# A two-layer trunk on one Trainium2 core: v of the second mixer in seven block products behind the first half of u, and gate of the first FFN in block products from the third group on

## The chip, the cores and the metric

The kernel runs on one core of one Trainium2 chip. A core has TensorE (PE in the profile; its weight loads are a row of their own, PEld), VectorE (DVE), ScalarE (ACT), GpSimd (POOL) and a queue engine that issues most of the loads (SP). The metric is device time of one execution in microseconds. Each engine runs its own queue of instructions strictly in order; engines wait for each other by semaphores.

## The reference

A sequence of 512 positions with 1024 channels goes through two layers and a last norm, all in 32-bit floats. Each layer is a mixer and a gated FFN, both with a residual around them.

```python
def gated_conv_ffn(x, w_gate, w_up, conv_w, conv_b, w_down):      # D_FF = 2816
    g = causal_dwconv3(x @ w_gate, conv_w) + conv_b
    return (silu(g) * (x @ w_up)) @ w_down

# mixer of layer 1 (C_WIDTH = 1024, CHUNK = 128, 8 heads of 128 channels)
proj = gelu(rms_norm(h, norm_mix[1]) @ w_in_odd)                  # 1024 -> 2048
u, v = proj[..., :C_WIDTH], proj[..., C_WIDTH:]
vn   = rms_norm(v, sgu_norm).reshape(b, n, CHUNK, C_HEADS, C_HEAD_DIM)
gate = einsum('hts,bnshc->bnthc', w_spatial * tril, vn) + b_spatial
h    = h + (u * gate.reshape(b, s, C_WIDTH)) @ w_out_odd
```

Layer 0's mixer (a gated short convolution and multi-scale pooling) is not touched but for the pools its buffers lie in.

## The kernel before

**Products.** Every 32-bit operand is split into a high part (rounded by a copy on ScalarE) and a low part (the rest, by a subtraction). A product is three matmuls, high x high, high x low and low x high (`mm3`). The split of a weight is written in two ways: `parts` (L125 to L130) has the high part on ScalarE (L128) and the low part on VectorE (L129); `summed` (L115 to L123) has ScalarE write the negated rounded value (L120), a DMA from GpSimd's queue add the raw weight on it (L121), and ScalarE write the high part (L122). Raw weights come by SP's queue (`fetch`, L109) into four buffers; high and low parts have six each. Larger temporary sums have the tag "sum" in the stage's own pool, three buffers.

**Order.** The program is written as a sequence of calls, and a planner (a list scheduler with costs of its own) sets from it the order in each engine's queue. The changed code can therefore come out in another order than it is written in.

**Stages.** Layer 0's mixer, layer 0's FFN, layer 1's mixer, layer 1's FFN.

**FFN.** The 2816 hidden channels are 22 blocks of 128, taken in groups of two (f = 0, 2, ... 20). For each group gate and up are computed, gate goes through the causal convolution (ScalarE L506, VectorE L508) and silu (L519), is multiplied with up, and split (`act`). The table PARTS runs a down projection (`project`, 512-column matmuls, residual additions at L292) after groups 2, 4, 8, 12, 16 and 20. Three forms of a group are there:

- `direct` (groups 0 and 2): full products.
- `both` (groups 4, 6, 10, 14, 18): gate and up each in seven block products in the manner of Strassen and Winograd. The activations' block sums are made once (`normalize`); weights' block sums s12 and s34 are made per group. Each block product is 12 matmuls of 256 columns (`multiply`, L638), so a group has 2 x 84. The products of gate and up alternate; results are copied out by ScalarE (L696) or added by VectorE (L701 to L721). Three PSUM banks (a, b, e) serve each of gate and up, and are used again within the group.
- `seven` (groups 8, 12, 16, 20): up in seven block products, gate in 48 full matmuls of 512 columns.

So a `both` group has always stood behind a down projection, and a `seven` group behind a `both` group, but for group 4, which follows a down projection and is followed by one.

**Layer 1's mixer.** `in_group` computes half of v or u: 512 columns of w_in_odd, four tiles of 128 tokens, 8 x 4 x 3 = 96 matmuls of 512 columns. The order is v0, v1, then v's norm, u0, the eight spatial products, u1 with transposes between, the gating, and the output projection oo. `tail` is how many of the eight contraction steps are run tile by tile at the end (with a large tail the tiles finish one after the other, with a small one together). The spatial weights are masked by GpSimd and turned by TensorE (L877) while v0 runs, in two sets of four.

Of the kernel before, what the change touches and what calls it, by code (L numbers as in the profile page):

```python
# [8 lines left out]
F32 = mybir.dt.float32  # L9
F32R = mybir.dt.float32r  # L10
# [5 lines left out]
P = 128  # L16
# [14 lines left out]
def tile_trunk(ctx: ExitStack, tc: tile.TileContext, x, norm_mix, norm_ffn, final_norm,  # L31
# [301 lines left out]
    def mixer0():  # L333
        nonlocal prm0
        w = w_in_even[0]
        with tc.tile_pool(name="m0", bufs=1) as mp:
# [5 lines left out]
            def load(k, n):  # L342
                t = mp.tile([P, NT, n * P], F32, tag="four", bufs=5, name=f"xt{k}")
# [90 lines left out]
            def c_done(j, ps):  # L434
                if j % 2 == 0:
                    ac["pair"] = mp.tile([P, 2, S], F32, tag="four", bufs=5, name=f"ac{j}")
# [9 lines left out]
            def v_done(j, ps):  # L446
                p = padded_tile()
                nc.vector.tensor_tensor(p[:, 2:], ps, ac[j], ALU.mult)
                if j % 2 == 0:
                    cv["pair"] = mp.tile([P, 2, S], F32, tag="four", bufs=5, name=f"cv{j}")  # L450
# [37 lines left out]
    class Ffn:  # L488
# [33 lines left out]
        def act(self, ft, s):  # L522
            if ft == NF - 2 and self.kept:
                both = self.ap.tile([P, 2, S], F32R, tag="sum", bufs=3, name="a_last")
# [56 lines left out]
        def normalize(self, kp):  # L581

            n, r = f"{self.layer}_{kp}", self.r
            x = self.ap.tile([P, 2, S], F32, tag="sum", bufs=3, name=f"x{n}")
# [12 lines left out]
            t = self.ap.tile([P, 4, HALF], F32, tag="sum", bufs=3, name=f"t{n}")  # L597
            nc.vector.tensor_tensor(t[:, 1, :], b22, b12, ALU.subtract)
            nc.vector.tensor_tensor(t[:, 0, :], t[:, 1, :], b11, ALU.add)
            nc.vector.tensor_tensor(t[:, 3, :], b12, b11, ALU.subtract)  # L600
            nc.vector.tensor_tensor(t[:, 2, :], b21, t[:, 0, :], ALU.subtract)
            self.t23[kp] = self.sums(kp)
            t41 = self.ap.tile([P, 2, 2, HALF], F32R, name=f"t41_{n}")
            self.t41[kp] = t41[:, 0], t41[:, 1]
            for (hi, lo), src in ((self.t23[kp], t[:, :2, :]), (self.t41[kp], t[:, 2:, :])):
                if kp < 2:
                    halves((hi, lo), src)
                    continue
                nc.scalar.activation(lo, src, AF.Copy, scale=-1.0)
                nc.gpsimd.dma_start(lo, src, accum_op=ALU.add)  # L610
                nc.scalar.activation(hi, src, AF.Copy)
# [38 lines left out]
        def both(self, f):  # L650
# [12 lines left out]
            for key in "gu":  # L663
                r0, r1 = raws[key, 0][0], raws[key, 1][0]
                s12, s34 = (ap.tile([P, 2, 4, P], F32, tag="sum", bufs=3, name=f"{x}{key}_{n}")
                            for x in ("s12", "s34"))
# [57 lines left out]
        def seven(self, f, steps=None):  # L724
# [16 lines left out]
            gate = [parts(*raws["g", 0])]  # L741
            s23 = ap.tile([P, 2, 4, P], F32, tag="sum", bufs=3, name=f"s23_{n}")
            s14 = ap.tile([P, 2, 4, P], F32, tag="sum", bufs=3, name=f"s14_{n}")
            nc.vector.tensor_tensor(s14[:, 0], r0[:, :, P:], r1[:, :, P:], ALU.add)
# [77 lines left out]
        def hidden(self, f, before=lambda i, j: None, steps=None):  # L822
# [37 lines left out]


    def mixer1(norm):
        w = w_in_odd[0]
        with tc.tile_pool(name="m1", bufs=1) as mp:
# [6 lines left out]
                                    compare_op=ALU.is_ge, fill=0.0, base=0, channel_multiplier=1)  # L871
            wsT_hi = mp.tile([P, NK, P], F32R, name="wsT_hi")
            wsT_lo = mp.tile([P, NK, P], F32R, name="wsT_lo")
            for q in range(2):
                ps = aux_bank(f"wst{q}")
                for i in range(4):
                    nc.tensor.transpose(ps[:, i * P : (i + 1) * P], ws[:, 4 * q + i, :], ident)  # L877
                hi = wsT_hi[:, 4 * q : 4 * q + 4, :]
                pv = ps.rearrange("p (h t) -> p h t", t=P)
                nc.scalar.activation(hi, pv, AF.Copy)  # L880
                nc.vector.tensor_tensor(wsT_lo[:, 4 * q : 4 * q + 4, :], pv, hi.bitcast(F32),
                                        ALU.subtract)

# [9 lines left out]

            def v_done(half):
                def done(t, ps):
                    dst = v[t][:, half * 512 : (half + 1) * 512]
                    nc.scalar.activation(dst, ps, AF.Gelu, scale=r_of(t))
                    sq = tp.tile([P, S], F32, tag="sq", name=f"sqv{half}_{t}")
                    nc.scalar.activation(sq, dst, AF.Square, accum_out=ssv[:, half, t : t + 1])
# [18 lines left out]

            u, gt, mix = {}, {}, {}

            def u_done(half):
                u[half] = mp.tile([P, NT, S], F32, tag="u", bufs=2, name=f"u{half}")

                def done(t, ps):
                    nc.scalar.activation(u[half][:, t, :], ps, AF.Gelu, scale=r_of(t))
                return done

            def by_chunk(ap):
                return ap.rearrange("p (n c) -> p n c", c=P)

            def spatial(j):
                ps = mm_bank(f"sp{j}")
                cs = slice(j % 4 * P, (j % 4 + 1) * P)
                mm3(ps, (wsT_hi[:, j, :], wsT_lo[:, j, :]),
                    (vn[j // 4][0][:, :, cs], vn[j // 4][1][:, :, cs]), True, True)
# [8 lines left out]
            def gated(j):  # L944
                nc.vector.scalar_tensor_tensor(
                    gt[j], gt[j], prm1("bsp", j), u[j // 4][:, :, j % 4 * P : (j % 4 + 1) * P],
                    op0=ALU.add, op1=ALU.mult)

# [24 lines left out]
            for j in range(4, 8):  # L973
# [12 lines left out]
    def ffn1(norm):  # L986
        with tc.tile_pool(name="f1", bufs=1) as ap:
# [31 lines left out]
            def down(a):  # L1019
# [28 lines left out]
                def t_tile(i):  # L1048
                    return ap.tile([P, 2, 512], F32, tag="sum", bufs=3, name=f"t{i}_{a}")

# [150 lines left out]
```

## Time and profile before

| What | us |
|---|---|
| median of 3 runs | 996.63 |
| lowest and highest | 996.44, 997.19 |
| the profiled execution | 995.47 |
| its span, first to last instruction | 993.7 |
| TensorE busy | 982.4 (99%) |
| TensorE weight loads busy | 857.3 (86%) |
| VectorE busy | 719.3 (72%) |
| ScalarE busy | 527.9 (53%) |
| GpSimd busy | 100.8 (10%) |

The profile shows one execution. Its page gives busy times, the chain of work that ended last, the costliest groups of instructions by line and operands, and the DMA issues. From the trace come TensorE's waits, tables of busy times by window, and the chain or the instructions in order of time. A matmul's duration in the groups of lines (390 ns for 512 columns) includes the pipeline; what it costs in a row of matmuls is the distance between two starts. The granted clock of TensorE was 0.997 of full speed.

### The profile page before, as it was taken

To read this page: it belongs to the slowest core of one execution; us is meant where nothing else is said; L and a number is where in the kernel's file an instruction comes from. 1 tells how busy PE (TensorE), PEld (TensorE's weight loads), DVE (VectorE), ACT (ScalarE), POOL (GpSimd) and SP (SyncE) were. 2 spreads that over 40 slices of the span, in tenths; PEclk is the share of its full clock that TensorE was granted. 3 is DMA by queue.
4 is the path that set the end of the run, shared out by engine and by line. 5 is a ranking of instruction groups with operands and counts; after the bars stand their busy time and mean duration, and the time that the engine had idled before them with its cause. 6 is when DMAs were issued, how large, how long until landed. Compare 5 with 4: busy or idle time off the path is not lost.

```text
span 993.7 us, 14101 instructions
## 1 busy us (share of the span) xinstructions
PE 982.4 (99%) x5499; PEld 857.3 (86%) x5499; DVE 719.3 (72%) x1065; ACT 527.9 (53%) x767; POOL 100.8 (10%) x117
## 2 busy tenths in 40 slices
PE   9999999999999999999999999999999999999997
PEld 6788888898989989899888888888998988989885
DVE  5977457968675676755842546479789989898996
ACT  6523345744543636446555534567566557565752
POOL 3032030300000000000210001203001001000000
PEclk9999999999999999999999999999999999999998
DMA  7532224454355443544342212335555646566332
GB/s 241 177 107 84 85 85 128 106 151 126 112 143 148 114 121 107 148 130 117 137 148 70 100 64 86 106 106 117 137 148 131 165 145 144 149 156 174 121 92 85
DMA packets 83950, 124.50 MB, mean 125 GB/s; under 512 B 4292, under 2 KB 53676, under 8 KB 83884
## 3 DMA queue, kind: packets, MB, share of 16 engines
q1 hardware_dynamic: 75628, 98.96, 30.4%
q0 software_dynamic: 6912, 23.07, 12.7%
q10 hardware_dynamic: 1344, 1.58, 0.5%
q8 instruction: 43, 0.70, 0.3%
q14 instruction: 23, 0.19, 0.1%
HBM read 98.42 MB, written 2.10 MB: 101 GB/s over the span
## 4 chain that ended last, share of the span: by engine, by line
PE 93%; issue 3%; DVE 2%; ACT 1%; DMA 0%; POOL 0%; DVEq 0%; ACTq 0%; POOLq 0%
PE d L133 4%; PE d L135 4%; PE d L134 4%; PE g L133 3%; PE g L134 3%; PE g L135 3%; PE gu L133 2%; PE gu L135 2%; PE gu L134 2%; PE v L133 1%; PE oo L135 1%; PE u L133 1%; PE u L134 1%; PE oo L134 1%; PE u L135 1%
## 5 line engine op out<-in xcount | busy, mean ns | idle before, releaser
L134 PE MATMUL d<-a_lo,whi_d 128*128 128x512 f32 x176 | 68.6, 390 | 0.0
L135 PE MATMUL d<-a_hi,wlo_d 128*128 128x512 f32 x176 | 68.6, 390 | 0.0
L508 DVE SCALAR_TENSOR_TENSOR c<-rows,prm,c 128x512 f32<-128x512 f32 x88 | 67.4, 777 | 0.1
L133 PE MATMUL d<-a_hi,whi_d 128*128 128x512 f32 x176 | 67.1, 391 | 0.0
L133 PE MATMUL g<-hgh,whi_g 128*128 128x512 f32 x128 | 50.0, 391 | 0.0
L134 PE MATMUL g<-hgl,whi_g 128*128 128x512 f32 x128 | 50.0, 391 | 0.0
L135 PE MATMUL g<-hgh,wlo_g 128*128 128x512 f32 x128 | 49.8, 389 | 0.0
L129 DVE TENSOR_TENSOR wlo_d<-raw_d,whi_d 128x1024 fp32r<-128x1024 f32 x22 | 26.7, 1219 | 30.2 <-ACT whi_d L128 30.2
L129 DVE TENSOR_TENSOR wlo_u<-raw_u,whi_u 128x1024 fp32r<-128x1024 f32 x16 | 19.5, 1222 | 34.2 <-ACT whi_u L128 34.1
L121 POOL DMA_DIRECT2D wlo_u<-raw_u x18 | 15.4, 858 | 265.3 <-ACT wlo_u L120 182.9
L292 DVE TENSOR_TENSOR h<-d,h 128x512 f32<-128x512 f32 x48 | 32.4, 685 | 11.9 <-PE d L135 11.7
L134 PEld LDWEIGHTS d<-a_lo,whi_d 128*128 128x128 f32 x176 | 33.1, 188 | 7.1 <-DVE a_lo L249 0.2
L133 PEld LDWEIGHTS d<-a_hi,whi_d 128*128 128x128 f32 x176 | 33.0, 188 | 6.9
L135 PEld LDWEIGHTS d<-a_hi,wlo_d 128*128 128x128 f32 x176 | 33.0, 188 | 6.8
L519 ACT ACTIVATE s<-c,prm 128x512 f32<-128x512 f32 x44 | 31.5, 717 | 10.0 <-DVE c L508 9.8
L129 DVE TENSOR_TENSOR wlo_g<-raw_g,whi_g 128x1024 fp32r<-128x1024 f32 x20 | 24.4, 1219 | 14.0 <-ACT whi_g L128 14.0
L189 POOL TENSOR_TENSOR ssq_f<-ssq_f,sq_f 128x512 f32<-128x512 f32 x12 | 16.3, 1358 | 179.8 <-ACT sq_f L188 144.9
L175 ACT ACTIVATE hgh<-h,prm 128x512 fp32r<-128x512 f32 x24 | 17.3, 720 | 32.0 <-DVE h L292 32.0
L176 DVE SCALAR_TENSOR_TENSOR hgl<-h,prm,hgh 128x512 fp32r<-128x512 f32 x24 | 22.1, 922 | 15.0 <-ACT hgh L175 14.9
L128 ACT ACTIVATE whi_d<-raw_d 128x1024 fp32r<-128x1024 f32 x22 | 23.2, 1055 | 17.7 <-PE g L134 14.0
L506 ACT ACTIVATE c<-rows,prm 128x512 f32<-128x512 f32 x44 | 31.6, 719 | 1.6 <-DVE rows L701 1.0
L128 ACT ACTIVATE whi_g<-raw_g 128x1024 fp32r<-128x1024 f32 x20 | 21.0, 1051 | 19.9 <-PE u_18a L638 4.2
(1130 smaller groups left out, 3439.6 us busy)
## 6 DMA issues: line engine op xcount, KB each, us to landing
raw_g<-in_w_ffn_gate_dram SPq DMA_DIRECT2D x36, 512.0 KB, 3.8
raw_u<-in_w_ffn_up_dram SPq DMA_DIRECT2D x36, 512.0 KB, 3.5
raw_d<-in_w_ffn_down_dram SPq DMA_DIRECT2D x22, 512.0 KB, 3.5
raw_dn<-in_w_ffn_down_dram SPq DMA_DIRECT2D x22, 512.0 KB, 3.6
wlo_u<-raw_u POOLq DMA_DIRECT2D x18, 512.0 KB, 5.2
wlo_g<-raw_g POOLq DMA_DIRECT2D x14, 512.0 KB, 4.6
raw_oe<-in_w_out_even_dram SPq DMA_DIRECT2D x8, 512.0 KB, 3.5
raw_g<-in_w_ffn_gate_dram SPq DMA_DIRECT2D x16, 256.0 KB, 2.9
```

The source lines that it names most:

```text
L128: nc.scalar.activation(hi, raw, AF.Copy)
L129: nc.vector.tensor_tensor(lo, raw, hi.bitcast(F32), ALU.subtract)
L133: order(nc.tensor.matmul(ps, lhs[0], rhs[0], start=start, stop=False))
L134: nc.tensor.matmul(ps, lhs[0], rhs[1], start=False, stop=False)
L135: nc.tensor.matmul(ps, lhs[1], rhs[0], start=False, stop=stop)
L175: nc.scalar.activation(hg[k][0], h[k], AF.Copy, scale=g)
L176: nc.vector.scalar_tensor_tensor(hg[k][1], h[k], g, hg[k][0].bitcast(F32), op0=ALU.mult, op1=ALU.subtract)
L189: nc.gpsimd.tensor_tensor(self.ssq, self.ssq, sq, ALU.add)
L292: nc.vector.tensor_tensor(h[k], ps, h[k], ALU.add)
L506: nc.scalar.activation(c, t[:, 0:S], AF.Copy, scale=prm("cf", ft))
L508: self.convolved = nc.vector.scalar_tensor_tensor(c, t[:, i : S + i], prm("cf", i * NF + ft), c, op0=ALU.mult, op1=ALU.add)
L519: nc.scalar.activation(s, c, AF.Silu, bias=self.prm("bf", ft))
```

## The change

1. Layer 0's FFN: groups 8, 12, 16 and 20 are computed by `both`. In group 20 the second raw weights of gate and up are split by `parts`, not `summed`.
2. Layer 1's mixer: u0 goes first, with a tail of 2. Then v goes in seven block products (`v_blocks`). The block sums of weights are made on VectorE in place (`sums_of`), those of the normalised activations by `sum_rows` from h and the gain; products 7 and 4 split their weights by `summed`, the others by `parts`. The block b22 of the weights is loaded a second time. Each product is 2 x 4 x 3 = 24 matmuls of 512 columns; results are copied out by ScalarE (`keep`) or added by VectorE. `turn_spatial` is called between products 2 and 6. u1 follows with a tail of 1, the spatial products between its contraction steps 4 and 5 and the first transposes between steps 6 and 7. The gating is split in two instructions per head.
3. The tag "sum" is in one pool for all stages; mixer 0's five buffers of the tag "four" become two, and three of "sum".

```diff
@@ Ffn.both
-                hi, lo = summed(*raws[key, 1])
+                hi, lo = (parts if f == NF - 2 else summed)(*raws[key, 1])
@@ Ffn.hidden
-            elif f % 4 == 2 or f == 4:
+            elif f % 4 == 2 or f == 4 or self.layer == 0:
                 self.both(f)
             else:
                 self.seven(f, steps)
@@ new, called by mixer1
+    def v_block(w, r, c, i):
+        t = (wp.tile([P, 2, S], F32, tag="sum", bufs=3, name=f"v{r}{c}_{i}") if c else
+             wp.tile([P, 2, S], F32, tag="raw", bufs=4, name=f"raw_v{r}{c}_{i}"))
+        ...
+    def v_blocks(mp, w, v, v_gelu, loads, turn_spatial):
+        ...
+        def give(product, i, raw, by_dma=False):
+            mov[product, i] = (summed if by_dma else parts)(raw, 2, S, f"v{product}_{i}")
+        ...
+        def sum_rows(kp):
+            k, l = kp, kp + NP
+            gk, gl = prm1("mix", k), prm1("mix", l)
+            ...
+            nc.vector.tensor_scalar_mul(t, h[l][:, b], gl)
+            stt = nc.vector.scalar_tensor_tensor
+            stt(x[:, 0], h[k][:, b], gk, t, op0=ALU.mult, op1=ALU.add)
+            stt(x[:, 1], h[k][:, a], gk, x[:, 0], op0=ALU.mult, op1=ALU.subtract)
+            stt(y[:, 0], h[l][:, a], gl, x[:, 1], op0=ALU.mult, op1=ALU.add)
+            nc.vector.tensor_tensor(y[:, 1], x[:, 1], t, ALU.add)
+            for n, src in ((0, x), (2, y)):
+                hi, lo = (sums[kp][:, m, n : n + 2] for m in range(2))
+                nc.scalar.activation(hi, src, AF.Copy)
+                nc.vector.tensor_tensor(lo, src, hi.bitcast(F32), ALU.subtract)
+        ...
+        def multiply(product, at, on_done):
+            for i in range(2):
+                ...
+                for kp in range(NP):
+                    hi, lo = stat(product, kp, i)
+                    whi, wlo = (x[:, kp % 2, :] for x in mov[product, kp // 2])
+                    for l, r, end in ((hi, whi, False), (hi, wlo, False),
+                                      (lo, whi, kp == NP - 1)):
+                        nc.tensor.matmul(ps, l, r, start=first, stop=end, skip_group_check=True)
+                        first = False
+                on_done(i, ps)
+        ...
+        def sums_of(i):
+            give(2, i, b21[i])
+            minus(b11[i], b12[i], b11[i])
+            minus(b12[i], b22[i], b12[i])
+            minus(b22[i], b11[i], b22[i])
+            nc.vector.tensor_tensor(b21[i], b21[i], b22[i], ALU.add)
+
+        multiply(1, "a", keep(0, 0))
+        sums_of(0)
+        sums_of(1)
+        for kp in range(NP):
+            sum_rows(kp)
+        for i in range(2):
+            give(6, i, b22[i])
+        last = [v_block(w, 1, 1, i) for i in range(2)]
+        multiply(2, "b", c11)
+        for i in range(2):
+            give(5, i, b11[i])
+        turn_spatial()
+        multiply(6, "a", keep(0, 1))
+        for i in range(2):
+            give(7, i, b12[i], True)
+        multiply(5, "e", lambda i, ps: None)
+        multiply(7, "a", c22)
+        for i in range(2):
+            give(3, i, last[i])
+            give(4, i, b21[i], True)
+        multiply(3, "e", c12)
+        multiply(4, "a", lambda i, ps: v_gelu(2 + i, 0, ps))
@@ mixer1
-            in_group("v0", w, 1024, False, v_done(0), 2)
-            in_group("v1", w, 1536, False, v_done(1), 4)
+            in_group("u0", w, 0, False, u_done(0), 2)
+            v_blocks(mp, w, v, v_gelu, v_loads(w), turn_spatial)
@@ mixer1
-            in_group("u0", w, 0, False, u_done(0), 4)
-            for j in range(NK):
-                spatial(j)
-                if j < 4:
-                    gated(j)
-
             def first_half(k):
-                if 2 <= k < 6:
-                    turned(k - 2)
-
-            in_group("u1", w, 512, False, u_done(1), 4, before=first_half)
+                if 4 <= k < 6:
+                    for j in range(4 * k - 16, 4 * k - 12):
+                        spatial(j)
+                        if j < 4:
+                            gated(j)
+                elif k >= 6:
+                    turned(2 * k - 12)
+                    turned(2 * k - 11)
+
+            in_group("u1", w, 512, False, u_done(1), 1, before=first_half)
             for j in range(4, 8):
                 gated(j)
```

More of the change, by code (lines that the diff above doesn't have):

```diff
@@ L449, in v_done @@
                 if j % 2 == 0:
-                    cv["pair"] = mp.tile([P, 2, S], F32, tag="four", bufs=5, name=f"cv{j}")
+                    cv["pair"] = wp.tile([P, 2, S], F32, tag="sum", bufs=3, name=f"cv{j}")
                 t = cv["pair"][:, j % 2, :]
@@ new lines, in v_blocks, with minus, stat, row @@
+    def v_blocks(mp, w, v, v_gelu, loads, turn_spatial):
+        def minus(dst, a, b):
+            nc.vector.tensor_tensor(dst, a, b, ALU.subtract)
+        mov = {}
+        def give(product, i, raw, by_dma=False):
+            mov[product, i] = (summed if by_dma else parts)(raw, 2, S, f"v{product}_{i}")
+        b11, b12, b21, b22 = ([loads[r, c, i] for i in range(2)]
+                              for r, c in ((0, 0), (0, 1), (1, 0), (1, 1)))
+        for i in range(2):
+            give(1, i, b11[i])
+        sums = [mp.tile([P, 2, 4, HALF], F32R, tag="vn", bufs=4, name=f"vs{kp}")
+                for kp in range(NP)]
+        a, b = slice(0, HALF), slice(HALF, S)
+        AT = {5: 0, 6: 1, 3: 2, 7: 3}
+        def sum_rows(kp):
+            k, l = kp, kp + NP
+            gk, gl = prm1("mix", k), prm1("mix", l)
+            x, y = (tp.tile([P, 2, HALF], F32, tag="rstd", name=f"vx{n}_{kp}") for n in range(2))
+            t = tp.tile([P, S], F32, tag="sq", name=f"vt{kp}")[:, :HALF]
+            nc.vector.tensor_scalar_mul(t, h[l][:, b], gl)
[8 more added lines that the diff above has]
+                nc.vector.tensor_tensor(lo, src, hi.bitcast(F32), ALU.subtract)
+        def stat(product, kp, i):
+            ts_ = slice(i * P, (i + 1) * P)
+            if product in AT:
+                return tuple(sums[kp][:, n, AT[product], ts_] for n in range(2))
+            k = kp if product == 1 else kp + NP
+            c = slice(i * P + (HALF if product == 4 else 0),
+                      (i + 1) * P + (HALF if product == 4 else 0))
+            return tuple(x[:, c] for x in hg[k])
+        banks = {}
+        def multiply(product, at, on_done):
+            for i in range(2):
+                first = (at, i) not in banks
+                if first:
+                    banks[at, i] = mm_bank(f"v{at}{i}")
+                ps = banks[at, i]
+                for kp in range(NP):
[6 more added lines that the diff above has]
+                on_done(i, ps)
+        def row(t, half):
+            return v[t][:, half * S : (half + 1) * S]
+        def add(dst, ps):
+            nc.vector.tensor_tensor(dst, ps, dst, ALU.add)
+        def keep(t0, half):
+            return lambda i, ps: nc.scalar.copy(row(t0 + i, half), ps)
+        def c11(i, ps):
+            add(row(i, 0), ps)
+            v_gelu(i, 0, row(i, 0))
+        def c12(i, ps):
+            add(row(i, 1), ps)
+            v_gelu(i, 1, row(i, 1))
+        def c22(i, ps):
+            nc.scalar.copy(row(2 + i, 1), ps)
+            add(row(2 + i, 1), banks["e", i])
+            v_gelu(2 + i, 1, row(2 + i, 1))
+        def sums_of(i):
[21 more added lines that the diff above has]
+        multiply(7, "a", c22)
+        for i in range(2):
+            give(3, i, last[i])
+            give(4, i, b21[i], True)
+        multiply(3, "e", c12)
+        multiply(4, "a", lambda i, ps: v_gelu(2 + i, 0, ps))
@@ L871, in mixer1, with turn_spatial @@
                                     compare_op=ALU.is_ge, fill=0.0, base=0, channel_multiplier=1)
[L872 to L882, printed above, removed]
+            wsT = []
+            def turn_spatial():
+                wsT.append(mp.tile([P, NK, P], F32R, name="wsT_hi"))
+                wsT.append(wp.tile([P, NK, P], F32R, tag="sum", bufs=3, name="wsT_lo"))
+                wsT_hi, wsT_lo = wsT
+                for q in range(2):
+                    ps = aux_bank(f"wst{q}")
+                    for i in range(4):
+                        nc.tensor.transpose(ps[:, i * P : (i + 1) * P], ws[:, 4 * q + i, :], ident)
+                    hi = wsT_hi[:, 4 * q : 4 * q + 4, :]
+                    pv = ps.rearrange("p (h t) -> p h t", t=P)
+                    nc.scalar.activation(hi, pv, AF.Copy)
+                    nc.vector.tensor_tensor(wsT_lo[:, 4 * q : 4 * q + 4, :], pv, hi.bitcast(F32),
+                                            ALU.subtract)
             rcol = []
@@ L933, in spatial @@
                 cs = slice(j % 4 * P, (j % 4 + 1) * P)
-                mm3(ps, (wsT_hi[:, j, :], wsT_lo[:, j, :]),
+                mm3(ps, (wsT[0][:, j, :], wsT[1][:, j, :]),
                     (vn[j // 4][0][:, :, cs], vn[j // 4][1][:, :, cs]), True, True)
@@ L944, in gated @@
             def gated(j):
-                nc.vector.scalar_tensor_tensor(
-                    gt[j], gt[j], prm1("bsp", j), u[j // 4][:, :, j % 4 * P : (j % 4 + 1) * P],
-                    op0=ALU.add, op1=ALU.mult)
+                for t in range(0, NT, 2):
+                    nc.vector.scalar_tensor_tensor(
+                        gt[j][:, t : t + 2, :], gt[j][:, t : t + 2, :], prm1("bsp", j),
+                        pairs[j // 4, t][:, :, j % 4 * P : (j % 4 + 1) * P],
+                        op0=ALU.add, op1=ALU.mult)
             def turned(j):
```

51 lines of the change are left out of this document (31 added, 20 removed).

## Prediction, made before the changed kernel was run

> **What bounds the kernel now.** I read first the page's busy shares and the shares of the chain that ended last, then TensorE's own waits, then windows cut at the edges of the stages that change.
>
> ```profile
> span 993.7 us, 14101 instructions
> ...
> PE 982.4 (99%) x5499; PEld 857.3 (86%) x5499; DVE 719.3 (72%) x1065; ACT 527.9 (53%) x767; POOL 100.8 (10%) x117
> ...
> PE 93%; issue 3%; DVE 2%; ACT 1%; DMA 0%; POOL 0%; DVEq 0%; ACTq 0%; POOLq 0%
> ```
>
> TensorE is busy 99% of the span and holds 93% of the last chain. The list of its waits has nothing large:
>
> ```profile
> PE clock L56 <- DVE idle L53: 1.3, 1, 1.3
> PE u_4e L638 <- DVE wlo_s12u L648: 0.6, 1, 0.6
> ...
> PE u_4a L638 <- ACT kept L696: 0.3, 1, 0.3
> ```
>
> (total, times, longest). So the kernel goes as its queue of matmuls goes: a matmul taken away is worth its spacing to the next, and anything added elsewhere costs nothing until TensorE waits for it. The spacings come from the windows and from runs of twelve matmuls in the chain in order of time:
>
> ```profile
> core 0: us, PE busy (x) PEld busy (x) DVE busy (x) ACT busy (x) POOL busy (x), PEclk, DMA share, GB/s
> 246.08:266.24 20.16, 20.16 (x171) 20.16 (x170) 11.24 (x17) 10.73 (x17) 0.85 (x1) 1.00 0.37 105
> 266.24:287.24 21.00, 21.00 (x134) 19.08 (x133) 14.51 (x22) 13.84 (x22) 0.85 (x1) 1.00 0.55 151
> 309.09:329.25 20.16, 20.16 (x171) 20.16 (x170) 11.24 (x17) 10.72 (x17) 0.85 (x1) 1.00 0.38 106
> 498.40:543.00 44.60, 44.60 (x206) 36.83 (x205) 15.11 (x18) 23.01 (x38) 3.78 (x3) 1.00 0.34 118
> 543.00:594.40 51.40, 51.40 (x237) 42.56 (x236) 25.91 (x39) 24.66 (x34) 0.00 (x0) 1.00 0.24 82
> ```
>
> ```profile
> 248.96 1.44 PE g_6e L638 x12
> 250.40 1.44 PE g_6a L638 x12
> ...
> 748.84 2.72 PE dn2a L1042 x12
> ```
>
> Twelve matmuls of 256 columns take 1.44 us, 0.120 each; twelve of 512 columns 2.72, 0.227 each. Rows 246.08 and 309.09 are FFN groups whose gate and up both go as block products: 2 x 84 matmuls of 256 columns, 168 x 0.120 = 20.16, the window exactly. Row 266.24 is a group with up in block products and gate in full products: 84 x 0.120 + 48 x 0.227 = 20.97 of 21.00. The last two rows are layer 1's mixer up to its output projection (v, then u and the spatial gate), also without a hole.
>
> **The change part by part: what leaves TensorE.**
>
> *Layer 0's FFN.* Groups 8, 12, 16 and 20 turn from the 21.00 us form to the 20.16 us form: 0.84 each, 4 x 0.84 = 3.36 us. By columns alone it would be 48 x 512 against 84 x 256, an eighth of 10.9 us or 1.36 a group; the rest is lost because a 256-column matmul costs more than half of a 512-column one. Why shows in the third figure of the rows: weight loads are busy 20.16 of 20.16 in the block form, 19.08 of 21.00 in the mixed one, so a 256-column matmul waits for the next load. [...]
>
> *Layer 1's v.* Two groups of 96 matmuls become seven block products of 24, all of 512 columns: 192 to 168, 24 x 0.227 = 5.44 us.
>
> u keeps its 192 matmuls, the spatial product its 24, transposes keep their number. Together -8.80 us.
>
> **What is added, and its cover.** The rows for prices: ScalarE's and POOL's timeline about the block-form group 10, the median landings from the page's DMA issues, then three of VectorE's groups of lines:
>
> ```profile
> 309.87 1.04 ACT L120 ACTIVATE wlo_u<-raw_u 128x1024 fp32r<-128x1024 f32 x1
> 310.82 0.35 ACT L696 COPY rows<-g_10a 128x256 f32<-128x256 f32 x1
> ...
> 326.83 1.04 ACT L128 ACTIVATE whi_g<-raw_g 128x1024 fp32r<-128x1024 f32 x1
> 327.77 1.04 ACT L647 ACTIVATE whi_s<-s 128x1024 fp32r<-128x1024 f32 x1
> 328.72 0.71 ACT L506 ACTIVATE c<-rows,prm 128x512 f32<-128x512 f32 x1
> 329.34 0.70 ACT L519 ACTIVATE s<-c,prm 128x512 f32<-128x512 f32 x1
> ```
>
> ```profile
> 311.21 0.85 POOL L121 DMA_DIRECT2D wlo_u<-raw_u  x1 [11.38 <-ACT rows L696]
> ```
>
> ```profile
> raw_u<-in_w_ffn_up_dram SPq DMA_DIRECT2D x36, 512.0 KB, 3.5
> ...
> wlo_u<-raw_u POOLq DMA_DIRECT2D x18, 512.0 KB, 5.2
> ```
>
> ```profile
> L701 DVE TENSOR_TENSOR kept<-u_6e,kept 128x256 f32<-128x256 f32 x1 | 0.4, 413 | 0.0
> ```
>
> ```profile
> L129 DVE TENSOR_TENSOR wlo_u<-raw_u,whi_u 128x1024 fp32r<-128x1024 f32 x16 | 19.5, 1222 | 34.2 <-ACT whi_u L128 34.1
> ...
> L292 DVE TENSOR_TENSOR h<-d,h 128x512 f32<-128x512 f32 x48 | 32.4, 685 | 11.9 <-PE d L135 11.7
> ```
>
> *FFN, a block-form group right behind another.* Today each block-form group follows a down projection, whose TensorE time covers the preparation; now groups 8, 12, 16 and 20 follow one directly. ScalarE and VectorE have room in sum: about 11 us each of 20.16. The order decides. In the changed kernel's queue gate's product 6 takes over the PSUM bank of product 1, so it needs ScalarE's copy of that. Ahead of the copy on ScalarE stand, from 0.09 us after the group's start (first silu, 329.34 against 329.25): two silu (0.62 apart, 328.72 to 329.34), four 1024-wide copies (0.94 apart, 326.83 to 327.77) and two 512-wide activation copies (at most 0.62): 0.09 + 1.24 + 3.76 + 1.24 = 6.33, with the copy's 0.35 6.7. The planner has put 55 matmuls ahead of it, due at 55 x 0.120 = 6.6. Up's second product needs the low part that POOL adds by DMA: its ScalarE copy ends at about 6.1 here, issue follows 0.3 later (310.91 to 311.21), landing 5.2 later: 11.6, against a due time of 11.8 (98 matmuls). Both are even. Bounds: 0, where the order holds, to 0.9 a group, the sum of the two rows of such waits above (u_4e and u_4a, a block-form group too). A gain is excluded: a wait can't be negative. I take 0.2, nearer nothing because both come out within 0.2 of due: 4 x 0.2 = 0.8. Behind the copy on ScalarE wait the other drains of this group, which the later products give 1.44 us each. In group 20 the two low parts that POOL would add go to VectorE (2 x 1.22 us): covered by the 9 us that VectorE is idle in such a group.
>
> The mixer's other prices are groups of the lines between 498.4 and 594.4 us:
>
> ```profile
> L899 ACT ACTIVATE sqv<-v 128x512 f32<-128x512 f32 x8 | 5.0, 631 | 0.1
> L925 ACT ACTIVATE u<-u,rc_m1c 128x512 f32<-128x512 f32 x7 | 4.8, 690 | 10.2 <-PE u L135 10.2
> ...
> L881 DVE TENSOR_TENSOR wsT_lo<-wst,wsT_hi 128x512 fp32r<-128x512 f32 x2 | 1.4, 692 | 1.7 <-ACT wsT_hi L880 1.7
> ```
>
> *Mixer, u's first half first.* The 22 us of it (96 x 0.227 = 21.8) stand where v0 stood and need the same normalised input; the raw loads (3.5 us) are queued as those of v0 were. Its cost is nothing, and it gives the sums of v 22 us of cover. Without that cover the eight weight sums (below) would stand in the open, 8 x 1.13 = 9 us.
>
> *Mixer, VectorE.* By spacing (a little under the busy time; I take 1.13, 0.60 and 0.34 us for 1024, 512 and 256 columns) the new work is 10 low parts and 8 sums of weights, 18 x 1.13 = 20.3; sums of activation rows, four times (5 x 0.34 + 2 x 0.60) = 11.6; six additions of products, 3.6. With what stays (u's low parts, the turned spatial weights) some 42 us, from the start of u0 to the seventh product 22.6 + 6 x 5.44 + 1.3 = 57 us later. It fits, with 15 us over. ScalarE's share of that stretch: 18 copies of 1024 columns at 0.94, 8 of 512 and 8 drains at 0.62, 16 gelu and squares at 0.66, 37 us. POOL issues four accumulating transfers for products 7 and 4, whose raw sums are ready 10 us ahead of the matmuls, against 5.2 for the landing. SP has two more loads of 512 KB at 3.5 us in a stage where the DMA share is 0.34 and 0.24.
>
> *Mixer, turned spatial weights.* Four transposes between the second product and the third (6), four after 15 matmuls of the fourth (5). The second set takes over what the first left, so it waits for VectorE's low part of the first, which is queued behind a weight's low part and its ScalarE copy. I walk the two queues with the spacings above to 42.0 us after u0's start; the transposes are due at 42.75. Product 5's other 9 matmuls and everything behind wait if that fails. Cost 0.1; bound 1.3, the wait if one more 1024-wide copy and low part come first (0.94 + 1.13 less the 0.75 of slack).
>
> *Mixer, end of u1.* u1's tail goes from 4 to 1, so its four gelu of 0.69 bunch behind the last matmul; the split gate product and the first transposes that need them reach the output projection at 93.0 of 93.5 us by the same walk. Bounds 0 to 2.1 (three gelu); I take 0.2.
>
> The buffers that move between pools are the same in number; mixer 0, the early FFN groups and layer 1's FFN keep their order on every engine. Nothing.
>
> **Sum**: -3.36 - 5.44 + 0.8 + 0.3 = -7.7 on the profiled execution, 995.47 (span 993.7 and 1.77 around it): 987.8. That execution lies 1.16 us under the median 996.63, so the median comes to 988.9.
>
> **The rivals.**
>
> *FFN gives its gain back, mixer pays.* The copy of the first gate product or the POOL transfer is 0.8 to 1.2 us later than walked: 3.2 to 4.8 lost, 991.5 to 993. For: both slacks are about 0.1. Against: the planner moved gate's product 6 from the fourth place, where row 250.40 would have it due at 4.3 us, to 6.6, and the waits seen are 0.6 at most.
>
> *FFN waits are long.* If ScalarE's chain runs 2.4 us behind the matmuls, as it would with product 6 in its old place at 4.3 us (it could through late drains of the group before), each group loses 6.7 - 4.3 = 2.4 us, 9.6 in all: 997.7, no gain or a small loss.
>
> *Mixer gives it back, FFN pays*: 996.63 - 3.36 + 0.8 = 994.1, if the waits in v reach 5.4 us: one late slot release that shifts a product by its own length.
>
> *Slower: VectorE becomes the bound in v.* Rows of VectorE beside a POOL add:
>
> ```profile
> 499.43 1.54 DVE L129 TENSOR_TENSOR wlo_v<-raw_v,whi_v 128x1024 fp32r<-128x1024 f32 x1
> 500.90 1.78 DVE L176 SCALAR_TENSOR_TENSOR hgl<-h,prm,hgh 128x512 fp32r<-128x512 f32 x1
> ```
>
> 1.54 against the 1.22 above, and 1.78 for a 512-wide instruction. If the 42 us of VectorE work, or the waits of its queue behind ScalarE's copies, stretch by 1.6, that is 67 us in 57: 10 us more, 988.9 + 10 = 999. It decides from (57 + 7.7)/42 = 1.54 times. For: the order is fixed, a low part waits for its ScalarE copy, that for a slot which a matmul frees, and by my walk ScalarE is busy nearly end to end from 24 to 40 us. Against: the slow rows lie beside POOL's two last adds alone, and none stands later. [...]
>
> *No effect* needs one of the waits above to cancel the 8.8 us by chance, and has no case of its own.
>
> **How the numbers follow.** Forecast 0.55; FFN given back 0.13; mixer given back 0.06; long FFN waits 0.08, half of it within 0.2% (2 us, about what this measurement can tell from no change); VectorE-bound v and other late chains there 0.18. Faster 0.55 + 0.13 + 0.06 = 0.74, same 0.04, slower 0.18 + 0.04 = 0.22. Likeliest alone: 987.0 (no waits, 987.8, less the spread of 0.1%) to 991. The range reaches to 998.5, which leaves out most of the last case and little below: 0.15 to 0.2.
>
> **What would show it.** Windows of groups 8, 12, 16, 20 at 20.16 us with weight loads busy throughout; if wrong, holes before gate's product 6, named after ScalarE's copy, or before up's second, after a DMA. The stretch from the end of layer 0's last down projection to the output projection: 96.0 - 5.4 = 90.6 us; if wrong, TensorE waits named after VectorE low parts or ScalarE high parts of v, or at the second set of transposes. The prediction falls if spacings differ: block matmuls of v over 0.227 us, or 256-column ones over 0.120 where nothing waits.

## The result, and the profile after

The changed kernel took 994.76 us (median of 9 runs, 993.88 to 995.91) against 997.06 (9 runs, 996.37 to 998.63): ratio 0.9978, 95% interval 0.9968 to 0.9988. It is faster, by 2.3 us; 7.7 us were forecast on the medians (996.63 to 988.9). The time lies inside the range; the gain is less than a third of the forecast.

The page of the profiled execution (995.75 us, 1.0 above the median):

```profile
span 994.0 us, 14507 instructions
...
PE 976.8 (98%) x5619; PEld 859.3 (86%) x5619; DVE 767.4 (77%) x1151; ACT 552.9 (56%) x809; POOL 107.7 (11%) x123
...
PE 84%; DVE 7%; issue 4%; ACT 3%; DMA 1%; POOL 0%; SPq 0%; DVEq 0%; ACTq 0%; POOLq 0%
```

TensorE's busy time fell by 5.6 us, but the span did not: TensorE's share of the chain that ended last went from 93% to 84%, VectorE's from 2% to 7%. TensorE's own waits (total, times, longest) name the places:

```profile
PE wst L1008 <- DVE wsT_lo L1012: 2.7, 1, 2.7
PE xt_ps L358 <- DMA xt<-in_x_dram: 2.0, 1, 2.0
PE sp L133 <- DVE gt L1072: 1.8, 1, 1.8
```

Windows of the same execution (columns as in the prediction): one of the new block-form groups, the mixer up to its output projection, and the two holes in it with what follows each:

```profile
267.94:288.10 20.16, 20.16 (x169) 20.16 (x169) 14.66 (x22) 14.30 (x24) 0.86 (x1) 1.00 0.59 157
...
496.90:594.60 97.70, 93.14 (x419) 76.56 (x417) 70.98 (x106) 63.47 (x95) 9.43 (x8) 0.98 0.43 119
539.80:542.70 2.90, 0.17 (x2) 0.04 (x1) 1.92 (x2) 2.90 (x4) 0.45 (x2) 1.00 0.99 194
542.70:547.30 4.60, 4.60 (x16) 3.73 (x17) 0.69 (x1) 1.20 (x3) 0.45 (x1) 0.63 0.96 224
576.80:578.80 2.00, 0.17 (x2) 0.03 (x1) 2.00 (x4) 0.95 (x2) 0.00 (x0) 1.00 0.00 0
578.80:583.00 4.20, 4.20 (x18) 3.46 (x19) 4.20 (x10) 0.00 (x0) 0.00 (x0) 1.00 0.41 125
```

Cut at the same instructions, the two profiles differ so:

| Stretch | before | after | forecast |
|---|---|---|---|
| start to the third projection of layer 0's mixer | 81.9 | 83.7 | 0 |
| layer 0's FFN from group 6 on | 252.1 | 249.3 (-2.8) | -2.6 |
| layer 1's mixer up to its output projection | 96.4 | 97.7 (+1.3) | -5.1 |
| the rest to the end of layer 1's FFN | 391.1 | 391.3 | 0 |

The FFN gives what was forecast; the mixer gives nothing. (A second profile of the kernel before, shown below, has 97.0 us for the mixer, so the loss there is 0.7 to 1.3 us.) The mixer needs 91.0 us of matmuls (96.4 - 5.44) and took 97.7: 2.9 us of hole at the second set of turned spatial weights, 4.6 x (1 - 0.63) = 1.7 us because the granted clock is 0.63 behind that hole, and 2.0 us of hole at the spatial products, 6.6 of 6.7 us. The start is taken up below.

What ScalarE and VectorE did ahead of the first hole, by the timeline:

```profile
537.61 1.06 ACT L120 ACTIVATE wlo_v<-v 128x1024 fp32r<-128x1024 f32 x1
538.57 1.05 ACT L122 ACTIVATE whi_v<-v 128x1024 fp32r<-128x1024 f32 x1
539.52 1.05 ACT L128 ACTIVATE whi_v<-v 128x1024 fp32r<-128x1024 f32 x1
```

```profile
540.60 1.23 DVE L129 TENSOR_TENSOR wlo_v<-v,whi_v 128x1024 fp32r<-128x1024 f32 x1 [5.65 <-ACT whi_v L128]
541.86 0.69 DVE L1012 TENSOR_TENSOR wsT_lo<-wst,wsT_hi 128x512 fp32r<-128x512 f32 x1
```

VectorE is idle for 5.65 us in front of a low part of product 3 (540.60), since ScalarE reaches its high part only at 539.52, behind the two copies of product 7's `summed`. The low part of the turned spatial weights (541.86), whose PSUM bank TensorE waits for, stands behind that in VectorE's queue, and it does not pass it: its own high part was done at 536.6, in that idle time.

### The profile page after: what moved, and what is told of

Its sections match the earlier page's. It is cut to its first block, busy times and chain, and to the rows that moved or that the text cites. A ratio compares the mean times of both kernels' runs of the same rounds, so it can differ in the third digit from the quotient of the medians.

```text
span 994.0 us, 14507 instructions
## 1 busy us (share of the span) xinstructions
PE 976.8 (98%) x5619; PEld 859.3 (86%) x5619; DVE 767.4 (77%) x1151; ACT 552.9 (56%) x809; POOL 107.7 (11%) x123
## 4 chain that ended last, share of the span: by engine, by line
PE 84%; DVE 7%; issue 4%; ACT 3%; DMA 1%; POOL 0%; SPq 0%; DVEq 0%; ACTq 0%; POOLq 0%
PE d L133 4%; PE d L134 4%; PE d L135 4%; PE gu L133 2%; PE gu L134 2%; PE gu L135 2%; PE g L133 1%; PE g L134 1%; PE oo L133 1%; PE oo L135 1%; PE oo L134 1%; PE oe L135 1%; PE oe L133 1%; PE g L135 1%; PE oe L134 1%
## 5 line engine op out<-in xcount | busy, mean ns | idle before, releaser
L648 ACT ACTIVATE whi_s12u<-s12u 128x1024 fp32r<-128x1024 f32 x14 | 14.8, 1059 | 41.3 <-PE d L134 33.7
L121 POOL DMA_DIRECT2D wlo_g<-raw_g x17 | 14.8, 870 | 204.5 <-ACT wlo_g L120 172.3
L648 ACT ACTIVATE whi_s12g<-s12g 128x1024 fp32r<-128x1024 f32 x14 | 14.8, 1060 | 28.8 <-DVE s12g L669 22.3
L189 POOL TENSOR_TENSOR ssq_m<-ssq_m,sq_m 128x512 f32<-128x512 f32 x13 | 18.4, 1412 | 74.4 <-ACT sq_m L188 74.2
L128 ACT ACTIVATE whi_u<-raw_u 128x1024 fp32r<-128x1024 f32 x17 | 17.9, 1052 | 13.8 <-PE oe L134 4.4
```

The costliest lines, as they stand in the source:

```text
L121: nc.gpsimd.dma_start(lo, raw, accum_op=ALU.add)
L128: nc.scalar.activation(hi, raw, AF.Copy)
L189: nc.gpsimd.tensor_tensor(self.ssq, self.ssq, sq, ALU.add)
```

## The experiments

### The FFN's change alone

```diff
@@ kernel before
-                hi, lo = summed(*raws[key, 1])
+                hi, lo = (parts if f == NF - 2 else summed)(*raws[key, 1])
-            elif f % 4 == 2 or f == 4:
+            elif f % 4 == 2 or f == 4 or self.layer == 0:
```

> The kernel before with layer 0's groups 8, 12, 16 and 20 as block products and nothing else of the change. Theory A (the FFN part pays as forecast, and the mixer loses all): four windows of 20.16 in place of 21.00 us less the 0.4 us that group 20 still waits, 3.0 us under the kernel before, ratio 0.9970. Theory B (part of the gain is given back by waits that the mixer's change hides): 1 us or less under it, ratio over 0.9990.

Measured: 995.57 us, ratio 0.9985 (0.9977 to 0.9994), 1.5 us faster. Its window and that of a second profile of the kernel before, from group 6 to the mixer:

```profile
246.90:496.50 249.60, 249.18 (x1731) 233.32 (x1730) 189.67 (x281) 138.59 (x207) 17.75 (x18) 1.00 0.46 131
```

```profile
247.20:499.40 252.20, 252.20 (x1587) 229.00 (x1586) 170.13 (x247) 130.16 (x191) 16.24 (x16) 1.00 0.45 126
```

2.6 us by the windows, 0.6 to 2.3 by the runs. In this profile layer 1's FFN, which the edit does not touch, was 0.6 us longer; 0.4 of that is a wait of TensorE for ScalarE in its group 6, the rest stays open. The windows speak for theory A: groups 8, 12 and 16 give 0.8 each, and the stretch behind group 18 gives 0.1 to 0.4, as TensorE waits 0.3 to 0.6 for VectorE's addition to a row of gate in group 18 (`g_18e`). The time settles neither theory: A's ratio of 0.9970 lies outside the interval, and of B's, over 0.9990, the interval holds only the low end.

### The mixer's change alone

```diff
@@ changed kernel
-            elif f % 4 == 2 or f == 4 or self.layer == 0:
+            elif f % 4 == 2 or f == 4:
```

> The changed kernel with layer 0's groups 8, 12, 16 and 20 as before (up in block products, gate full), so the mixer's change alone. Theory A (mixer's stretch 97.7 us against 96.4): 0.5 to 1.5 us over the kernel before, ratio 1.0005 to 1.0015. Theory B (the mixer gains too, and the profiled execution's later start of 1.7 us is part of the change, not chance): 0 to 2 us over, with the first matmuls of the layer-0 mixer again 1.7 us late; under A they are late by less than 0.5 in this profile.

Measured: 997.01 us, ratio 1.0000 (0.9991 to 1.0008). The mixer's change is worth nothing as it stands. The holes are there (1.6 and 1.7 us), shorter than with the FFN's change and with no drop of the clock behind either: the stretch is 95.4 us. The time fits the low end of both theories. The start was late again (83.8 us to the third projection, 81.9 in the first profile), so this run does not tell them apart; the last section of the experiments places the start.

### The second transposes in a bank of their own

```diff
-                    ps = aux_bank(f"wst{q}")
+                    ps = (aux_bank, mm_bank)[q](f"wst{q}")
```

> One line of the changed kernel: the second set of turned spatial weights goes to a PSUM bank of its own, so it no longer waits for VectorE to read the first, and the planner puts both sets between products 2 and 6. Theory A (where the second set stands is the cause): the 2.9 us hole goes, and with it the 1.7 us of slower clock behind it; 4.6 us under the changed kernel, 990.2 us, ratio to before 0.9932. Theory B (ScalarE is the bound of v, busy without a gap from 525 to 543 us): the hole returns before product 7 or 3, less than 1.5 us gained, 993 or more, ratio over 0.996.

Measured: 994.88 us, ratio 0.9984 (0.9976 to 0.9993), no gain over the changed kernel. The hole at the transposes is gone, but another took its place, and the mixer takes 97.9 us. TensorE's waits, the chain in order of time, and ScalarE's timeline:

```profile
PE ve L933 <- DVE v L941: 3.1, 2, 2.6
PE sp L133 <- DVE gt L1072: 1.6, 1, 1.6
...
PE va L933 <- DMA wlo_v<-v: 0.8, 1, 0.8
```

```profile
535.25 7.57 DMA wlo_v<-v
542.88 4.96 DMA v<-in_w_in_odd_dram
547.96 0.92 issue
548.88 1.04 ACT wlo_v L120
```

```profile
547.92 1.06 ACT L128 ACTIVATE whi_v<-v 128x1024 fp32r<-128x1024 f32 x1 [4.46 <-DMA v<-in_w_in_odd_dram]
```

This is not ScalarE's work, as theory B had it, but a chain of buffers. For product 7, POOL's transfer adds the raw sum onto the negated copy, so the sum's buffer is held until the transfer has landed (542.8). The second load of b22 takes that buffer, lands 5.0 us later, and ScalarE stands 4.46 us in front of that block's high part for product 3. Behind it in ScalarE's queue is the copy of a block of v, on which VectorE's addition waits, which frees the PSUM bank for product 3. Theory A's time falls for this edit alone. B's numbers came out (a hole ahead of product 3, over 993 us), but not its reason: ScalarE stands idle here for a load.

### Product 7's low parts by VectorE

```diff
-            give(7, i, b12[i], True)
+            give(7, i, b12[i])
```

> The changed kernel with product 7's low parts made by VectorE and not by ScalarE's copy and POOL's transfer: two ScalarE copies (1.9 us) fewer ahead of the high part that the hole waits for, two low parts (2.3 us) more on VectorE, in the 5.7 us in which it is idle. Theory A: the hole shrinks by 1.9 or more, to 1.0 us or less, and is too short for the clock to drop (the 2.0 us hole at the spatial product shows no drop): 3.5 us under the changed kernel, 991.2, ratio 0.9943. Theory B (ScalarE's work as a whole bounds v): 1.9 gained, 992.9, ratio 0.996. Theory C (VectorE's whole work bounds v): no gain or a loss, 994.8 or more.

Measured: 993.11 us (992.95 to 993.34), ratio 0.9961 (0.9949 to 0.9973), 1.7 us under the changed kernel; the mixer takes 95.7 us. The opposite half went: no wait is left at the spatial products, and the one at the transposes is as long as ever, with a lower clock behind it (granted clock is the last figure but two):

```profile
PE wst L1008 <- DVE wsT_lo L1012: 3.1, 1, 3.1
```

```profile
537.20:540.60 3.40, 3.06 (x11) 2.54 (x12) 1.59 (x3) 1.65 (x2) 0.00 (x0) 0.66 0.46 171
```

The chain ahead of that hole, in order of time:

```profile
534.42 2.28 DVE wlo_v L129 x2
536.79 0.70 DVE wsT_lo L1012
537.53 0.66 PE wst L1008 x4
```

Product 7's two low parts now stand ahead of the spatial weights' low part in VectorE's queue. Even so that low part is done 40.9 us after u0's start, against 45.7 in the changed kernel. The hole is as long because the planner moved the second transposes forward too: TensorE comes to them 37.7 us after u0's start and no longer at 42.9. So theory A's number is wrong, but its reason, fewer copies ahead of the high part, was not tested at a fixed due time. The time is the one that theory B gave (992.9), so the time does not exclude B; the experiments that follow do. Theory C's number (994.8 or more) falls.

### Both edits

> The changed kernel with both edits: product 7's low parts by VectorE, and a PSUM bank of its own for the second set of turned spatial weights. Theory D (two chains in a row: the second transposes wait for VectorE, and behind them the second load of b22 waits for a buffer that product 7's transfer holds; each alone leaves the other): no hole over 0.6 us is left between u0 and the output projection, the stretch from g_18's first matmul to the output projection falls from 160.4 to 153.5 us, and the time to 988.5, ratio to before 0.992. Theory B (ScalarE and VectorE together bound v): 992 or more, with a new wait for a low or high part of v.

Measured: 988.64 us (987.86 to 988.73), ratio 0.9905 (0.9891 to 0.9920). The stretch of the mixer, and the largest waits of TensorE in the whole kernel:

```profile
497.00:587.70 90.70, 90.70 (x417) 75.44 (x416) 72.84 (x108) 61.47 (x93) 7.41 (x6) 1.00 0.40 116
```

```profile
PE clock L56 <- DVE idle L53: 1.3, 1, 1.3
PE u_4e L639 <- DVE wlo_s12u L649: 0.6, 1, 0.6
```

No hole is left in the mixer; 90.7 us are the 96.4 less the 24 matmuls (91.0). The bank alone left 97.9 us and product 7's low parts alone 95.7. So two waits in a row, either of which takes most of the gain, are shown to be the cause: theory D holds, within 0.2 us of the time it gave. Theory B (992 or more) falls. The kernel before had a median of 998.09 in this round of runs and 996.81 in the round before it, so times from different rounds compare to about 1 us: against the changed kernel both edits are worth 6.1 us by the medians, 7.3 by the ratios and 7.0 by the mixer's windows.

### The second load into other buffers

```diff
-    def v_block(w, r, c, i):
-        t = (wp.tile([P, 2, S], F32, tag="sum", bufs=3, name=f"v{r}{c}_{i}") if c else
+    def v_block(w, r, c, i, again=False):
+        t = (wp.tile([P, 2, S], F32, tag="sum", bufs=3, name=f"v{r}{c}_{i}") if c and not again else
...
-        last = [v_block(w, 1, 1, i) for i in range(2)]
+        last = [v_block(w, 1, 1, i, True) for i in range(2)]
```

with the bank of its own, and product 7 by POOL's transfer as in the change.

> The changed kernel with the second transposes in a bank of their own, product 7 still by POOL's transfer, and the second load of b22 in the buffers of the raw weights, which product 5 frees early, in place of those that product 7's transfer holds. Theory D: the 2.6 us and 0.5 us waits of the run with the bank alone go, as the high part of product 3 no longer waits for that load (it waited 4.5 us): 991.5, ratio 0.9945. Theory B (ScalarE's own work): the waits stay, as nothing is taken from ScalarE: 994.5 or more.

Measured: 993.17 us (990.98 to 994.47), ratio 0.9951 (0.9938 to 0.9963). Between the two theories' times; D's ratio of 0.9945 lies in the interval, and B's time of 994.5 or more is above every run. The mixer takes 96.5 us. The waits at product 3 are gone, so the buffer was their cause, as D says. What is left is at the spatial products, and the granted clock in the window behind it was 0.62:

```profile
PE sp L133 <- DVE gt L1072: 1.8, 1, 1.8
```

```profile
575.40:579.00 3.60, 3.60 (x10) 2.88 (x11) 3.60 (x9) 0.00 (x0) 0.00 (x0) 0.62 0.43 146
```

Here the raw buffers that the second load takes are late for u1's own raw weights: ScalarE waits 4.2 us for one of these loads, and v's norm and the spatial products come late. SP's longest wait for such a buffer, 7.5 us, is for a transfer of product 4, which holds its raw sum in the same way. The wait has moved, not gone.

### Product 4's low parts on VectorE too

```diff
-            give(7, i, b12[i], True)
+            give(7, i, b12[i])
...
-            give(4, i, b21[i], True)
+            give(4, i, b21[i])
```

with the bank of its own.

> As the run with both edits, and product 4's low parts on VectorE too: two more low parts (2.3 us) on VectorE, two copies fewer on ScalarE, no POOL transfer left in v. Theory D: within 1 us of the run with both edits, 988 to 989.5. Theory C (VectorE's work bounds v): 2 us or more slower than that run, 990.5 or more.

Measured: 987.83 us (987.50 to 988.96), ratio 0.9902 (0.9889 to 0.9915), the same as with both edits within the spread. The mixer is 90.7 us again:

```profile
496.30:587.00 90.70, 90.70 (x417) 75.45 (x416) 75.24 (x110) 59.68 (x90) 5.66 (x4) 1.00 0.32 105
```

VectorE is busy 75.2 of 90.7 us, ScalarE 59.7, and TensorE has no hole. Neither is the bound of this stretch, and theory C (990.5 or more) falls.

### Without GpSimd's mask

```diff
-            nc.gpsimd.affine_select(out=ws, in_=ws, pattern=[[0, NK], [-1, P]],
-                                    compare_op=ALU.is_ge, fill=0.0, base=0, channel_multiplier=1)
```

> The changed kernel without GpSimd's mask on the spatial weights (so the spatial product runs over the whole 128 x 128 block and not its lower triangle; the matmuls are the same in number and shape). In the changed kernel the mask took 2.19 us beside VectorE, whose first 256-column scale took 1.18 us beside it and 0.35 elsewhere, with VectorE busy 21.6 of the first 22.6 us. Theory E (VectorE's lateness in that stretch, made worse by GpSimd, passes through the token scale and u's gelu into ScalarE's queue and sets the hole): the hole at the second transposes shrinks by about the 0.8 us, to 1.9, and the time by 0.8 to 2.5 us (with the clock's drop), ratio to before 0.9955 to 0.997. Theory F (the hole is set by the transfers and buffers behind product 7 alone): the hole stays at 2.7 us, ratio 0.998.

Measured: 994.83 us, ratio 0.9980 (0.9970 to 0.9989), the changed kernel's time. The hole shrank by half of what theory E gave, and a wait of the kind seen with the bank alone appeared:

```profile
PE ve L933 <- DVE v L941: 3.4, 2, 2.9
PE wst L1006 <- DVE wsT_lo L1010: 2.3, 1, 2.3
```

Behind neither did the clock drop. The hole is 0.4 us shorter, but with the mixer's change alone, mask and all, it was 1.6, so the 0.4 is not shown to be the mask's; and the mask is not what costs the gain. What the profiles with this order of queues do show is that the hole goes with the token scale of u (`rc_m1c`): the scale comes 24.4, 24.9, 25.6 and 25.8 us after u0's start and the hole is 1.6, 2.3, 2.75 and 2.7 us (mixer's change alone, this run, the changed kernel's second and first profile). That is E's direction. On the hole E and F stay undecided; for the time F's number came out.

### Both kernels once more

> The kernel before, once more, for the spread of the start: its profiled execution reached the third projection of layer 0's mixer at 81.9 us, the six runs with the changed layouts or FFN at 82.7 to 83.8. If the start is chance, this one is at 82.5 to 84 and the rest of the profile is the same to 0.3 us a stage; if the changed buffers cost it, 81.9 again.

Measured: 997.46 us in one execution. It reached the third projection at 83.3 us, the first profile at 81.9, with waits for the first loads of x of 0.6 and 0.4 us. The other profiles with the same order there lie between 82.5 and 83.8. The start is chance; the profile of before that the prediction used had an early one, 1.4 us under this. Its mixer is 97.0 us, 0.6 over the first where 0.3 was expected, with a wait of 0.4 us for GpSimd's mask. The FFN stretch is the same to 0.1 us.

> The changed kernel, once more, for the spread of the hole and of the clock behind it: 2.7 us and a granted clock of 0.63 over the next 4.6 us in the first profile. If the drop follows any hole of that length, it is there again; if it hangs on where the hole lies, the same hole can be followed by full clock, and the time falls by 1.7 us.

Measured: 996.04 us in one execution, start at 82.5 us. Both holes are there, 2.75 and 1.80 us, and the clock dropped behind both:

```profile
541.50:546.00 4.50, 4.50 (x15) 3.76 (x16) 0.69 (x1) 0.79 (x2) 0.41 (x1) 0.62 0.92 218
...
579.00:583.00 4.00, 4.00 (x12) 3.13 (x11) 3.57 (x8) 0.00 (x0) 0.00 (x0) 0.57 0.20 76
```

The mixer took 99.1 us here and 97.7 in the first profile, with one more drop of the clock (4.0 x 0.43 = 1.7 us). Such drops may be a part of why the changed kernel's runs spread over 2 us; that is not shown, as the kernel before, which has no such holes, spreads over 2.3.

## Why the prediction was wrong

**What leaves TensorE: right.** Block-form groups take 20.16 us also where they follow another, with weight loads busy throughout. 24 matmuls at 0.227 us leave the mixer: 90.7 us with no hole, against the 91.0 that the sum gives. The 0.2 us allowed for the end of u1 were not needed in those runs.

**FFN waits: right in size, one cause not foreseen.** 0.8 us were allowed for four groups; 249.3 against 252.1 - 3.36 = 248.7 is 0.6 lost. Neither of the two even races (ScalarE's copy, POOL's low part) shows a wait over 0.2 us; half of the loss (0.3) is at group 18's row addition. That the two races held with slacks of 0.1 was luck as much as reading.

**Mixer, turned spatial weights: wrong, the step that failed first.** The prediction gave it 0.1 us, at most 1.3. It cost 2.9, and 1.7 behind it by the clock, which no bound held. The queue was walked rightly in its order (the low part of the spatial weights behind a weight's low part, behind a ScalarE copy, due at 42.75 us after u0's start: 539.65, and TensorE came there at 539.8). The walk had VectorE done at 42.0; it was done at 45.7 (542.56). Two things in the profile stand behind the 3.7 us. VectorE's first 22.6 us are 95% full (fourth figure of the row):

```profile
496.90:519.50 22.60, 22.60 (x105) 18.84 (x104) 21.55 (x30) 9.75 (x13) 5.96 (x4) 1.00 0.16 47
```

So the token scale that u's gelu needs came 25.8 us after the start, where u0's matmuls end at 22.6; and ScalarE had no room from 533 us on, so that product 7's two copies pushed the high part back. How much each is worth is argued and not shown: no run moves one of them alone. The prediction's totals (42 of 57 us) said that the work fits, and it does, but a due time is not met by an average.

**Mixer, "POOL issues four accumulating transfers" and SP's two loads: wrong, costed at nothing.** The sentence looked at when product 7 is due. It did not ask what else waits for the buffer that the transfer holds. With the first wait gone, the second load of b22, held by that buffer, gave back the same time. With the bank alone TensorE even waited 0.8 us for one of the transfers. The landings were also longer than the 5.2 us used, from the DMA issues between 530 and 560 us:

```profile
wlo_v<-v POOLq DMA_DIRECT2D x2, 512.0 KB, 6.4
wlo_v<-raw_v POOLq DMA_DIRECT2D x2, 512.0 KB, 7.0
```

**Spatial products: not foreseen.** 2.0 us at the fourth of them, where VectorE's product with the gain (`gt`) stands behind a low part of the output projection's weights. The chain of the changed kernel leads further back:

```profile
556.31 4.63 DMA raw_u<-in_w_in_odd_dram
561.02 1.06 ACT whi_u L128
...
571.59 4.33 DVE vnl L1056 x7
...
576.90 1.22 DVE wlo_oo L129
578.12 0.61 DVE gt L1072
```

v's norm is late because ScalarE waits 2.6 us for a load of u1's raw weights (561.02), and SP had waited 6.6 us to issue that load, for a transfer of product 4 that held the buffer. It is the same kind of wait as at product 3. No run takes product 4's transfers away alone; with both edits they stay and this hole is gone, so they cost only where the rest is late.

**VectorE beside POOL: the mask was not counted.** The prediction has the slow rows beside POOL's two last adds alone and none later. The two adds and the mask all lie in the 57 us up to the seventh product, and a slow row lies beside the mask too. VectorE and POOL of the changed kernel by the timeline:

```profile
501.26 2.20 DVE L879 TENSOR_TENSOR raw_v<-v,raw_v 128x1024 f32<-128x1024 f32 x1
...
505.18 1.18 DVE L900 TENSOR_SCALAR vt<-h,prm 128x256 f32<-128x256 f32 x1
```

```profile
500.99 1.38 POOL L189 TENSOR_TENSOR ssq_m<-ssq_m,sq_m 128x512 f32<-128x512 f32 x1 [0.85 <-ACT sq_m L188]
504.02 2.19 POOL L997 TENSOR_SCALAR_AFFINE_SELECT ws<-ws 128x1024 f32<-128x1024 f32 x1 [1.65 <-DMA ws<-in_w_spatial_dram]
```

A sum of weights takes 2.20 us beside the add and 1.22 elsewhere, a scale 1.18 beside the mask and 0.35 elsewhere. Without the mask the same scale took 0.34, so the 1.18 is the mask's doing; the time of the kernel did not fall for it.

**Rivals.** What came is the one called "mixer gives it back, FFN pays" (994.1 us, chance 0.06), in part with its reason, a late release of a slot; that its time is met so closely is luck, as 1.7 us of the loss are the clock's and 2.0 lie behind v. It had too little chance: the prediction had itself found a slack of 0.75 us at the end of a walk of 42 us over two engines, and an error of 10% in such a walk is 4 us. VectorE as the bound of v is excluded by the runs with both edits and with product 4's low parts on VectorE too, which have no hole with VectorE busier than in the changed kernel (72.8 and 75.2 us against 71.0).

## What to carry to other kernels

When work is taken from a full engine and given to idle ones, totals say whether it fits and queues say whether it comes in time: walk to each due time with the spacings seen under load, and take the error of the walk, not its slack, as the bound. A transfer that adds in place held its source until it landed, 7.57 us in the run with the bank alone; ask which load wants that buffer next. Two waits in a row hid each other: removing either one alone gave nothing or 1.7 us here, removing both some 6 to 7, so a null result for one edit does not clear its cause.

## What the runs showed of the hardware

Five holes of 1.8 to 3.1 us in TensorE's queue were followed by a lower granted clock, which cost another 1.2 to 1.7 us behind them (an estimate from the windows: 3.4 x 0.34 to 4.6 x 0.37). After holes of 2.7, 2.75, 1.8, 1.8 and 3.1 us the granted clock over the next 3.4 to 4.6 us was 0.63, 0.62, 0.57, 0.62 and 0.66; after others of 1.6, 1.7, 1.8, 2.3, 2.6 and 2.9 us it stayed at 1.00. The same hole of the same kernel (1.8 us at the spatial products) was followed by a drop in one execution and not in the other, so that length alone does not decide. The rows behind the two longest holes without a drop, in the runs with the bank alone and without the mask:

```profile
552.00:556.00 4.00, 3.37 (x13) 2.47 (x14) 2.04 (x4) 3.90 (x7) 0.00 (x0) 1.00 0.99 232
552.00:556.00 4.00, 3.45 (x15) 2.51 (x15) 2.31 (x3) 4.00 (x7) 0.00 (x0) 1.00 0.60 104
```
